# RWKV-7 and retention in one layer stack: an inverse whose blocks are turned on the chip, and a gate that is computed by tokens

## The chip, the cores and the metric

One core of a Trainium2 chip. The metric is the device time of one execution in microseconds; the kernel before was timed three times. Everything is float32; the large products run as fp32r, with each weight and each input split into a high and a low part. PE is the matrix engine (TensorE), DVE the vector engine (VectorE), ACT the scalar engine (ScalarE), SP the engine that issues most of the DMAs.

## What is computed

Three blocks on 256 tokens of width 1024. Block 1 is retention beside an RG-LRU; block 2 is local attention, convolution and pooling with an FFN; block 3 has two layers, each an FFN, a mixer, a cross attention and an FFN. The mixer of the first layer is RWKV-7, that of the second a gMLP. The three places that matter here, cut:

```python
# block 1
o_ret = group_norm_heads(chunkwise_retention(q, k, v)).reshape(B, T, RET_WIDTH)
y_ret = o_ret * jax.nn.silu(g_ret)
mixed = jnp.concatenate([y_ret, y_lru], axis=-1)      # times w_out
# RWKV-7: 16 heads of 64
g = jax.nn.sigmoid(xg @ g1) @ g2
def step(state, inp):                                 # over 256 tokens
    r_t, w_t, k_t, v_t, kk_t, b_t = inp
    sa = jnp.einsum('bhij,bhj->bhi', state, -kk_t)
    state = (state * w_t[:, :, None, :] + sa[..., None] * b_t[:, :, None, :]
             + v_t[..., :, None] * k_t[:, :, None, :])
    return state, jnp.einsum('bhij,bhj->bhi', state, r_t)
y = group_norm(y) * ln_w + ln_b
bonus = jnp.sum(r_h * k_h * r_k, axis=-1, keepdims=True) * v_h
return ((y + bonus) * g) @ w_o
# gMLP
u, v = jnp.split(jax.nn.gelu(h @ w_uv), 2, axis=-1)
v = rms_norm_3(v, v_norm)                             # then mixed over tokens by w_s
return (u * sv) @ w_o
```

## The kernel before

**The products.** A weight comes as blocks of 1 MB (128 x 2048) over SP's queue. Each half of a block is split on the chip: ACT casts it to the high part (L456), DVE subtracts for the low part (L459). `linear` works by features: per pair (m, k) two 128x256 products with the high and low part of the weight's column tile and one with the input's low part (L546 to L548), 3 x 8 x 8 = 192 for a 1024 x 1024 matrix. `linear_tok` works by tokens: 128x512 products (L563 to L565), 3 x 8 x 2 x 2 = 96 for the same matrix. Results stand in PSUM in banks of two kinds, "d" and "x", four of each, until ACT or DVE takes them out.

**The order.** Nothing is scheduled by a compiler: each engine runs its instructions in the order in which the Python text issues them, and an instruction that waits holds all behind it on its engine. `later(n, f)` puts f into the n-th step from now, `chain` spreads functions over the next steps, `soon` puts one behind the next step's products; `tick` and `tock` of a linear's step run what is due. `pump` issues loads and splits.

**Block 1.** The retention's output is computed by tokens (`orow`), normalized and left there. `in_gl` and `in_gr` are linears by features whose outputs go through `gate_out` (L1038): a product with the row factor r, Silu, a product with the LRU's output or with a tile of `orow` that PE has turned (`turned`, L1057, two 128x128 transposes a tile), and the split into high and low part of the input of `out1`.

**RWKV.** The state is carried over four pieces c of 64 tokens, for two halves of the heads (`chain(q)`, q = 0, 1). Within a piece a triangular system is solved with an inverse that is prepared for all 32 pairs (head, two pieces) at once. Its diagonal 32x32 blocks are made on DVE by forward substitution with one `column(s)` per column, 31 in all, on 128 partitions (`uy`: the first half u the triangles, the second y the inverse); they run among the steps of `rw_v`, four a step. `gather` (L1921) then writes y to DRAM and reads it back as `inv` with four DMAs (L1927), each block now a 32x32 tile across partitions; `inv` is cleared by POOL first. The off-diagonal block is made by `beside`: `across` (L1941) multiplies the coupling block with the block in place, `corner` (L1950) multiplies the result with the other block. `across` needs the first block transposed, which DVE does with eight 32x256 STREAM_TRANSPOSEs (L2158).

Around it stand, in the order of PE: the last products of `rw_v`, evicted by ACT into SV (`ev_v`, L2017); `direct(0)` and `direct(1)` of both chains (L2064); the output gate g (`gates`, four calls of 8 matmuls each, L1850 and L1851, evicted by ACT at L1852); `across` and `corner`; then the chain of pieces: for c = 0 to 3 `right` (R from the state, copied to Rs at L2072), `solve` (L2081) and `step` (new state, L2092 to L2094; outputs every second piece, `outs`). The group norm of the first half of the tokens (`normal(0)`) and its gating (`gated(m, 0)`) run within the chain by `later`. DVE makes the bonus products (`bonuses`, L1842) between the columns and the chain. The weights of `rw_o` follow at L2192 with the first result needed.

**gMLP.** After `gm_v` its output v (two tiles of 128x2048) is scaled by the norm's factor in four 128x1024 instructions (L374), then `gm_u` begins, whose steps use v as the products of `mix` from the second step on.

Of the kernel before, what the change touches and what calls it, by code (L numbers as in the profile page):

```python
# [172 lines left out]
def blocks_of(i):  # L173
# [128 lines left out]
class Net:  # L302
# [500 lines left out]
    def block1(self):  # L803
# [234 lines left out]
        def gate_out(k, ps, other):  # L1038
            g = self.tmp("t")
            nc.vector.tensor_mul(g, ps[:, :T], r)  # L1040
            o = {}

            def silu():
                o[0] = other()
                self.act(g, g, AF.Silu)

            def out():
                nc.vector.tensor_mul(g, o[0], g)
                self.split(g, yp.hi(k), yp.lo(k), lazy=True)
            self.chain(silu, out)  # L1050
        self.later(2, lambda: self.drop(th, w, rope))
        self.later(4, lambda: setattr(self, "keep", 2))
        self.linear("in_gl", xp, KD, 8, lambda m, ps: gate_out(m, ps, lambda: hl[:, m]), drain=False, late=0)
# [3 lines left out]
        def turned(m):  # L1057
            pt = self.psum("x")
            for t in range(2):
                nc.tensor.transpose(pt[:, t * P:(t + 1) * P], orow[:, t, m * P:(m + 1) * P], self.ident)  # L1060
            return pt[:, :T]
        self.linear("in_gr", xp, KD, 8, lambda m, ps: gate_out(8 + m, ps, lambda: turned(m)), late=0)
# [492 lines left out]
    def gmlp(self, st, nxt):  # L1555
# [19 lines left out]
        self.linear_tok("gm_v", xp, 4, ev_v, late=True)  # L1575
        sv, sr, sa = (self.tmp(n, 2, bufs=1) for n in ("sv", "sr", "sa"))
# [3 lines left out]
        for h in range(2):  # L1580
            for t in range(2):
                self.ts(v[t][:, h * D:(h + 1) * D], v[t][:, h * D:(h + 1) * D], sr[:, t:t + 1])
# [33 lines left out]
    def rwkv(self, st, nxt):  # L1616
# [221 lines left out]
        def bonuses(q, t):  # L1838
            for e in range(2):
# [81 lines left out]
        def gather():  # L1921
            inv.append(self.slot([P, 32, 64]))
            nc.gpsimd.memset(flat(inv[0]), 0.0)
            nc.sync.dma_start(dram[1], sq(uy[0][:, 1024:]))
            for n in (0, 2, 1, 3):
                s = blk[n]
                nc.sync.dma_start(inv[0][s, :, blk[n % 2]], dram[1][s].rearrange("q j t -> j q t"))  # L1927
        uy, inv = [], []

        def beside(i):  # L1930

            X = sq(uy[0][:, :1024])
# [3 lines left out]
            def across():  # L1936
                ps[0] = self.psum("x")
                for p in range(8):
                    hd, cp = divmod(8 * i + p, 2)
                    for n, c in ((0, 2 * cp + 1), (2, 2 * cp)):  # L1940
                        mm(ps[0][blk[n + 1], at(p)], Gh(hd)[blk[n], c, blk[n + 1]], X[blk[n], 8 * i + p],  # L1941
                           start=True, stop=True)
# [69 lines left out]
        self.later(3, lambda: zipped([lambda s=s: column(s) for s in range(31)] + [gather], 4))  # L2012
# [9 lines left out]
        nc.vector.tensor_copy(nn[:, 3], sums[0][:, 32:64].rearrange("p (s h) -> p s h", s=2))  # L2022
        bonus = nn[:, 3]
# [3 lines left out]
        for q in range(2):  # L2027
            for t in range(2):
                bonuses(q, t)

# [122 lines left out]
        for m in range(0, 8, 2):  # L2153
            gates(m)
        self.drop(*wl[1:])
# [15 lines left out]
        for c in range(4):  # L2171
            for f in range(1, 4):
                for ch in chains:
                    self.tick()
                    ch[f](c)
# [138 lines left out]
```

## Time and profile before

| | |
|---|---|
| median of 3 runs | 1789.21 us (1788.69 to 1789.83) |
| the profiled execution | 1788.29 us |
| its span, first to last instruction | 1786.3 us |
| mean granted clock of TensorE, share of full speed | 0.992 |
| PE busy | 1759.2 us, 98% of the span |
| DVE, ACT, POOL busy | 70%, 51%, 1% |
| DMA | 310.34 MB, mean 174 GB/s |

In the rows below a line of a timeline reads: start in us from the span's start, its length, engine, source line, operation, written and read tile, shape, number of instructions in the row, and in brackets the idle time ahead of it and the instruction whose end released it. A row of several instructions shows their sum in the second column or the stretch that they fill. A granted clock of 1.00 is 2.4 GHz, 0.50 is 1.2 GHz.

### The profile page before, as it was taken

Reading aid. Unit: us, or ns where it says so; the run is one execution under the profiler, and the core shown is the slowest. Engines: PE = TensorE matmul, PEld = TensorE weight load, DVE = VectorE, ACT = ScalarE, POOL = GpSimd, SP = SyncE. Lnnn points to the kernel's source line nnn. Section 1 sums busy time; section 2 is a strip of 40 time slices with the busy share of each in tenths; the row PEclk is TensorE's granted clock in tenths of the full one; section 3 lists DMA queues with packets and bytes.
Section 4 is the critical chain, followed back from the end, with each engine's and each line's share of the span. In section 5 each row is a group of like instructions: output and inputs, shape, how many; then the busy total and the mean of one; then the engine's idle time right before and its main releaser. Section 6 shows DMA issues by size and latency. Waiting matters only on the chain.

```text
span 1786.3 us, 27620 instructions
## 1 busy us (share of the span) xinstructions
PE 1759.2 (98%) x11142; PEld 1537.8 (86%) x11142; DVE 1252.6 (70%) x2292; ACT 914.1 (51%) x1550; POOL 9.8 (1%) x29
## 2 busy tenths in 40 slices
PE   8999999999999999999999999999999999999997
PEld 8899899899987888888688888888888899888886
DVE  7898888997757656678786865565556488675553
ACT  6878455665536544163235554444444555454451
POOL 0000000000000000000000000000000000000000
PEclk9999999999999999999989999999999999999999
DMA  8455445454653645603344454464445636345450
GB/s 321 143 189 202 170 157 216 165 185 166 211 207 129 210 173 185 258 25 119 96 167 163 168 188 165 165 236 170 162 181 191 240 119 236 142 169 185 165 189 24
DMA packets 55496, 310.34 MB, mean 174 GB/s; under 512 B 13728, under 2 KB 16841, under 8 KB 19145
## 3 DMA queue, kind: packets, MB, share of 16 engines
q1 hardware_dynamic: 54792, 304.39, 47.4%
q10 hardware_dynamic: 576, 4.19, 0.6%
q8 instruction: 87, 1.43, 0.3%
q14 instruction: 41, 0.33, 0.1%
HBM read 304.36 MB, written 4.21 MB: 173 GB/s over the span
## 4 chain that ended last, share of the span: by engine, by line
PE 89%; DVE 7%; ACT 2%; DMA 1%; issue 1%; SPq 0%; DVEq 0%; ACTq 0%
PE psd L544 17%; PE psd L548 14%; PE psd L563 10%; PE psd L565 10%; PE psd L564 10%; PE psd L546 6%; PE psd L547 6%; PE psx L544 2%; DVE s L459 2%; PE psd L2192 2%; PE psd L541 1%; PE psx L1455 1%; PE psx L548 1%; ACT s L367 1%; PE psx L1495 1%
## 5 line engine op out<-in xcount | busy, mean ns | idle before, releaser
L459 DVE TENSOR_TENSOR s<-s,s 128x1024 fp32r<-128x1024 f32 x524 | 627.1, 1220 | 169.3 <-ACT s L456 168.7
L548 PE MATMUL psd<-s,s 128*128 128x256 f32 x2336 | 655.8, 281 | 3.0 <-DVE s L459 2.8
L456 ACT CAST s<-s 128x1024 fp32r<-128x1024 f32 x524 | 532.1, 1046 | 180.0 <-PE psd L548 99.5
L544 PE MATMUL psd<-s,s 128*128 128x512 f32 x1392 | 491.2, 397 | 0.9 <-DVE s L630 0.9
L548 PEld LDWEIGHTS psd<-s,s 128*128 128x128 f32 x2336 | 442.8, 190 | 4.7 <-DVE s L459 4.2
L563 PE MATMUL psd<-s,s 128*128 128x512 f32 x816 | 323.7, 397 | 0.7 <-ACT s L367 0.7
L565 PE MATMUL psd<-s,s 128*128 128x512 f32 x816 | 318.6, 390 | 0.7 <-DVE s L370 0.7
L564 PE MATMUL psd<-s,s 128*128 128x512 f32 x816 | 317.8, 389 | 0.0
L544 PEld LDWEIGHTS psd<-s,s 128*128 128x128 f32 x1392 | 261.3, 188 | 63.4 <-DVE s L630 1.3
L546 PE MATMUL psd<-s,s 128*128 128x256 f32 x944 | 271.7, 288 | 1.0 <-ACT s L456 1.0
L547 PE MATMUL psd<-s,s 128*128 128x256 f32 x944 | 266.9, 283 | 0.0
L546 PEld LDWEIGHTS psd<-s,s 128*128 128x128 f32 x944 | 180.8, 192 | 2.7 <-ACT s L456 1.2
L565 PEld LDWEIGHTS psd<-s,s 128*128 128x128 f32 x816 | 153.1, 188 | 34.0 <-DVE s L370 1.3
L547 PEld LDWEIGHTS psd<-s,s 128*128 128x128 f32 x944 | 180.9, 192 | 0.1
L563 PEld LDWEIGHTS psd<-s,s 128*128 128x128 f32 x816 | 153.3, 188 | 31.2 <-ACT s L367 1.0
L564 PEld LDWEIGHTS psd<-s,s 128*128 128x128 f32 x816 | 153.4, 188 | 30.5
L1459 DVE TENSOR_TENSOR s<-psx,s 128x512 fp32r<-128x512 f32 x44 | 30.4, 691 | 94.7 <-ACT s L1461 79.2
L367 ACT ACTIVATE t<-psd,rc 128x256 f32<-128x256 f32 x88 | 41.5, 475 | 99.1 <-PE psd L565 96.7
L1461 ACT CAST s<-psx 128x512 fp32r<-128x512 f32 x40 | 23.5, 587 | 120.7 <-PE psx L1455 120.7
L370 DVE SCALAR_TENSOR_TENSOR t<-psd,rc,t 128x256 f32<-128x256 f32 x88 | 41.5, 482 | 47.5 <-ACT t L367 47.5
L367 ACT ACTIVATE t<-x 128x256 f32<-128x256 f32 x86 | 34.2, 407 | 68.4 <-DVE x L370 44.5
L367 ACT ACTIVATE s<-x,vecs 128x256 fp32r<-128x256 f32 (+1 forms) x80 | 40.2, 506 | 50.2 <-DVE x L1419 36.3
(382 smaller groups left out, 1818.1 us busy)
## 6 DMA issues: line engine op xcount, KB each, us to landing
s<-w_ffn_in SPq DMA_DIRECT2D x88, 1024.0 KB, 4.8
s<-w_ffn_out SPq DMA_DIRECT2D x44, 1024.0 KB, 4.7
s<-w_up SPq DMA_DIRECT2D x22, 1024.0 KB, 4.8
s<-w_out SPq DMA_DIRECT2D x12, 1024.0 KB, 5.0
s<-w_down SPq DMA_DIRECT2D x11, 1024.0 KB, 4.7
s<-w_xq SPq DMA_DIRECT2D x8, 1024.0 KB, 5.4
s<-w_xo SPq DMA_DIRECT2D x8, 1024.0 KB, 4.7
s<-w_gm_v SPq DMA_DIRECT2D x8, 1024.0 KB, 4.7
```

Of the source, the lines that this page charges most:

```text
L367: return self.nc.scalar.activation(out, in_, func, **kw)
L370: return self.nc.vector.scalar_tensor_tensor(out, in0, scalar, in1, op0=op0, op1=op1)
L456: self.nc.scalar.copy(hi, raw[:, s])
L459: self.nc.vector.tensor_sub(lo, raw[:, s], hi.bitcast(F32))
L544: mm(out, w[0], x.two(k), start=first, stop=False)
L546: mm(out[:, :T], w[0], x.hi(k), start=first, stop=False)
L547: mm(out[:, :T], w[0], x.lo(k), start=False, stop=False)
L548: mm(out[:, :T], w[1], x.hi(k), start=False, stop=last)
L563: mm(out, hi, w[0], start=first, stop=False)
L564: mm(out, hi, w[1], start=False, stop=False)
L565: mm(out, lo, w[0], start=False, stop=last)
L2192: mm(ps[:, :P], blocks[m // 2][j * P:(j + 1) * P][0], yo[:, k, o], start=k == 0, stop=k == KD - 1)
```

## The change

**Retention.** The weight of `in_gr` is laid out as that of `in_v`, and the linear is `linear_tok`. `ev_gr` takes a 128x512 bank out with Silu (ACT, the row factor as its scale) and multiplies it with `orow` (DVE). `turned` then turns the product with PE (16 transposes as before, in four banks of two tiles by two), ACT copies the high part and DVE subtracts for the low part, 128x2x256 each.

**gMLP.** A call of `_need` stands ahead of the scaling, for the first block of `gm_u`; in the built order no split moves by it. Of the four scalings those of the second half of v are put off by 3 and 4 steps.

**RWKV.** `gather` reads back only two of the four blocks by DMA. The whole y is transposed block by block on DVE into u (one 128x1024 STREAM_TRANSPOSE), from which `across` now reads; two more, 128x512, turn another view of y into two temporary tiles, and ACT copies the other two blocks from these into `inv` (four 32x512 copies, L1965 of the changed kernel). The eight 32x256 transposes go. The clearing of `inv` goes among the columns, the copy of the bonus too. `gates(0)` stands ahead of `across`, `gates(2)` behind `corner` and the first `right`, `gates(4)` and `gates(6)` at the pieces c = 1 and c = 2. Of the eight bonus products four stand between `across` and `corner`, four at steps of the chain. `normal(0)` runs in steps 12 to 18, `gated(m, 0)` in steps 19 to 24.

```diff
-        w[key] = _groups(part) if key == "in_v" else _tiles(part)
+        w[key] = _groups(part) if key in ("in_v", "in_gr") else _tiles(part)
...
+        def ev_gr(g, t, ps):
+            s = rows[t] = self.tmp("e", 512, bufs=4)
+            self.act(s, ps, AF.Silu, scale=rc[:, t:t + 1])
+            prod = lambda: nc.vector.tensor_mul(s, s, orow[:, t, g * 512:(g + 1) * 512])
...
+                for i in range(2):
+                    self.later(2 - g, lambda i=i: turned(g, i, pair))
+        def turned(g, j, s):
...
+                    nc.tensor.transpose(pt[:, i * T + t * P:i * T + (t + 1) * P], s[t][:, o:o + P], self.ident)
...
+            def out():
+                nc.scalar.copy(hi, both)
+                nc.vector.tensor_sub(lo, both, hi.bitcast(F32))
...
-        self.linear("in_gr", xp, KD, 8, lambda m, ps: gate_out(8 + m, ps, lambda: turned(m)), late=0)
+        self.linear_tok("in_gr", xp, 2, ev_gr, drain=False)
...
+                scaled = lambda v=v[t][:, h * D:(h + 1) * D], r=sr[:, t:t + 1]: self.ts(v, v, r)
+                if h:
+                    self.later(3 + t, scaled)
+                else:
+                    scaled()
...
         def gather():
-            inv.append(self.slot([P, 32, 64]))
-            nc.gpsimd.memset(flat(inv[0]), 0.0)
-            nc.sync.dma_start(dram[1], sq(uy[0][:, 1024:]))
-            for n in (0, 2, 1, 3):
-                s = blk[n]
-                nc.sync.dma_start(inv[0][s, :, blk[n % 2]], dram[1][s].rearrange("q j t -> j q t"))
+            u, y = uy[0][:, :1024], uy[0][:, 1024:]
+            d = [self.tmp("e", 512, bufs=4) for _ in range(2)]
+            nc.sync.dma_start(dram[1], sq(y))
+            nc.vector.transpose(u, y)
+            for n in (0, 2):
+                nc.sync.dma_start(inv[0][blk[n], :, blk[0]], dram[1][blk[n]].rearrange("q j t -> j q t"))
+            for i in range(2):
+                nc.vector.transpose(d[i], sq(y).rearrange("p j t -> p t j")[:, 16 * i:16 * i + 16])
+            for i in range(2):
+                for n in (1, 3):
+                    nc.scalar.copy(inv[0][blk[n], :, 32 + 16 * i:48 + 16 * i],
+                                   d[i][blk[n]].rearrange("p (t q) -> p q t", q=32))
...
-        for m in range(0, 8, 2):
-            gates(m)
...
-        for i in range(0, 32, 8):
-            for n in (0, 2):
-                nc.vector.transpose(uy[0][blk[n], 32 * i:32 * i + 256], inv[0][blk[n], i:i + 8, blk[0]])
+        gates(0)
         steps = [beside(i) for i in range(4)]
-        for n in range(2):
-            for st in steps:
-                st[n]()
+        for st in steps:
+            st[0]()
+        for q in range(2):
+            bonuses(q, 0)
+        for st in steps:
+            st[1]()
+        for ch in chains:
+            ch[1](0)
+        gates(2)
...
         for i, f in enumerate(normal(0)):
-            self.later(13 + i // 2, f)
+            self.later(12 + i, f)
         for m in range(8):
-            self.later(17 + m, lambda m=m: gated(m, 0))
+            self.later((19, 20, 21, 21, 22, 22, 23, 24)[m], lambda m=m: gated(m, 0))
+        for i, n in enumerate((3, 4, 9, 10)):
+            self.later(n, lambda i=i: bonuses(i % 2, 1, (i // 2,)))
...
+            if c in (1, 2):
+                gates(2 + 2 * c)
```

The order of ACT around the end of the columns, before. L2017 takes the products of `rw_v` out of the banks psd, L1852 the gate, L1944 the first result of `across`; psd_8432 and psd_8433 are the first 512 columns (heads 0 to 7, used by the chain q = 0) of both tiles of tokens, psd_8604 and psd_8605 the other 512 (heads 8 to 15, q = 1), which PE finishes last.

```order
L2017 COPY s_1063_8430<-psd_8432 64x512 x2
L2017 COPY s_1064_8431<-psd_8433 64x512 x2
L2017 COPY s_1063_8430<-psd_8604 64x512 x2
L2017 COPY s_1064_8431<-psd_8605 64x512 x2
L1852 COPY s_1133_8717<-psx_8718 128x512
L1852 COPY s_1133_8717<-psx_8724 128x512
L1852 COPY s_1133_8717<-psx_8730 128x512
L1852 COPY s_1133_8717<-psx_8736 128x512
L1944 COPY s_1069_8454<-psx_8750 32x256
```

And now. L2059 is the former L2017, L1879 the former L1852, L1983 the former L1944; L1965 are the new copies into `inv`.

```order
L2059 COPY s_1051_8298<-psd_8300 64x512 x2
L2059 COPY s_1052_8299<-psd_8301 64x512 x2
L1965 COPY s_1103_8491<-e_8518 32x32x16 x2
L1965 COPY s_1103_8491<-e_8519 32x32x16 x2
L2059 COPY s_1051_8298<-psd_8473 64x512 x2
L2059 COPY s_1052_8299<-psd_8474 64x512 x2
L1879 COPY s_1123_8584<-psx_8585 128x512
L1983 COPY s_1057_8322<-psx_8591 32x256
L1983 COPY s_1057_8322<-psx_8610 32x256
```

The four copies, which read the tiles that DVE turns behind the last column, now stand ahead of the last two evictions of `rw_v`.

The order of PE from the last matmuls of the gate on, before: L1850 and L1851 are `gates`, L1941 `across`, L1950 `corner`, L2081 the first `solve`.

```order
L1851 MATMUL psx_8736<-s_900_7405,s_899_7404 128x256
L1941 MATMUL psx_8750<-s_1069_8454,s_1017_8067 32x32 x16
L1941 MATMUL psx_8769<-s_1069_8454,s_1038_8209 32x32 x16
L1941 MATMUL psx_8788<-s_1069_8454,s_1052_8329 32x32 x16
L1941 MATMUL psx_8807<-s_1069_8454,s_1060_8414 32x32 x16
L1950 MATMUL psx_8826<-s_1122_8645,s_1069_8454 32x32 x16
L1950 MATMUL psx_8845<-s_1122_8645,s_1069_8454 32x32 x16
L1950 MATMUL psx_8864<-s_1122_8645,s_1069_8454 32x32 x16
L1950 MATMUL psx_8883<-s_1122_8645,s_1069_8454 32x32 x16
L2081 MATMUL psx_8909<-s_1124_8676,s_1122_8645 64x64
```

And now, again from the last matmuls of the first call of `gates` on: L1877 and L1878 are `gates`, L1980 `across`, L1989 `corner`.

```order
L1877 MATMUL psx_8585<-s_888_7273,s_887_7272 128x256
L1878 MATMUL psx_8585<-s_888_7273,s_887_7272 128x256
L1980 MATMUL psx_8591<-s_1057_8322,s_1005_7935 32x32 x16
L1980 MATMUL psx_8610<-s_1057_8322,s_1026_8077 32x32 x16
L1980 MATMUL psx_8629<-s_1057_8322,s_1040_8197 32x32 x16
L1980 MATMUL psx_8648<-s_1057_8322,s_1048_8282 32x32 x16
L1989 MATMUL psx_8671<-s_1103_8491,s_1057_8322 32x32 x16
L1989 MATMUL psx_8690<-s_1103_8491,s_1057_8322 32x32 x16
L1989 MATMUL psx_8709<-s_1103_8491,s_1057_8322 32x32 x16
L1989 MATMUL psx_8728<-s_1103_8491,s_1057_8322 32x32 x16
L1877 MATMUL psx_8751<-s_888_7273,s_887_7272 128x256
L1878 MATMUL psx_8751<-s_888_7273,s_887_7272 128x256
```

Only one of the four calls of `gates` is left ahead of `across`; the second (psx_8751) stands between `corner` and the first `solve`, and calls three and four (not shown) stand in the chain.

The order of DVE where `gm_u` begins, before: L374 are the scalings, L459 is the low part of a half block of weights, L1602 the first product of `gm_u` with the row factor.

```order
L374 TENSOR_SCALAR s_1672_13050<-s_1672_13050,sr_13349 128x1024
L374 TENSOR_SCALAR s_1673_13051<-s_1673_13051,sr_13349 128x1024
L374 TENSOR_SCALAR s_1672_13050<-s_1672_13050,sr_13349 128x1024
L374 TENSOR_SCALAR s_1673_13051<-s_1673_13051,sr_13349 128x1024
L459 TENSOR_TENSOR s_1709_13340<-s_1704_13291,s_1709_13340 128x1024
L1602 TENSOR_TENSOR t_13394<-psd_13365,rB_13044 128x256
```

And now (L1629 is the former L1602):

```order
L374 TENSOR_SCALAR s_1662_12917<-s_1662_12917,sr_13216 128x1024
L374 TENSOR_SCALAR s_1663_12918<-s_1663_12918,sr_13216 128x1024
L459 TENSOR_TENSOR s_1699_13207<-s_1694_13158,s_1699_13207 128x1024
L1629 TENSOR_TENSOR t_13259<-psd_13230,rB_12911 128x256
L459 TENSOR_TENSOR s_1706_13255<-s_1694_13158,s_1706_13255 128x1024
L1629 TENSOR_TENSOR t_13296<-psd_13261,rB_12911 128x256
L459 TENSOR_TENSOR s_1711_13288<-s_1697_13190,s_1711_13288 128x1024
L374 TENSOR_SCALAR s_1662_12917<-s_1662_12917,sr_13216 128x1024
```

Two of the scalings moved behind the first three low parts.

## Rows read from the trace of the kernel before

**Rows 1.** The page of the profile, its parts 1 and 2 (busy time; slices)

```profile
PE 1759.2 (98%) x11142; PEld 1537.8 (86%) x11142; DVE 1252.6 (70%) x2292; ACT 914.1 (51%) x1550; POOL 9.8 (1%) x29
...
PEclk9999999999999999999989999999999999999999
```

**Rows 2.** Waits of TensorE in the whole span: total us, times, longest us

```profile
PE psd L548 <- DVE s L459: 2.8, 4, 1.6
...
PE psx L2138 <- DVE s L2131: 1.1, 1, 1.1
...
PE psx L2081 <- ACT s L2072: 0.9, 1, 0.9
PE psd L2058 <- ACT s L2072: 0.9, 2, 0.4
```

**Rows 3.** Busy time by stretch, end of in_v and end of in_gl; columns in the first line

```profile
core 0: us, PE busy (x) PEld busy (x) DVE busy (x) ACT busy (x) POOL busy (x), PEclk, DMA share, GB/s
52.24:63.36 11.12, 11.12 (x50) 9.18 (x49) 5.14 (x8) 10.90 (x22) 0.00 (x0) 1.00 0.54 195
142.29:151.00 8.71, 8.71 (x75) 8.71 (x74) 7.50 (x22) 7.82 (x22) 0.00 (x0) 1.00 0.20 59
```

**Rows 4.** Timeline of VectorE, then of TensorE, where gm_u begins

```profile
1432.66 2.74 DVE L374 TENSOR_SCALAR s<-s,sr 128x1024 f32<-128x1024 f32 x4
1435.32 1.22 DVE L459 TENSOR_TENSOR s<-s,s 128x1024 fp32r<-128x1024 f32 x1
...
1434.67 0.28 PE L547 MATMUL psd<-s,s 128*128 128x256 f32 x1
1436.59 0.39 PE L548 MATMUL psd<-s,s 128*128 128x256 f32 x1 [1.64 <-DVE s L459]
```

**Rows 5.** Timeline of VectorE and SyncE queue around the end of the columns

```profile
869.08 0.21 DVE L1919 TENSOR_TENSOR s<-s,t 128x31 f32<-128x31 f32 x1
869.21 0.18 DVE L2022 COPY rwn<-psx 128x32 f32<-128x32 f32 x1
869.38 0.32 SPq L1924 DMA_DIRECT2D inv_dram<-s  x1
869.49 5.71 DVE L1842 TENSOR_TENSOR s<-s,rwn 64x512 f32<-64x512 f32 x8
...
875.23 3.69 DVE L2158 STREAM_TRANSPOSE s<-s 32x256 f32<-32x256 f32 x8
```

**Rows 6.** Timeline of ScalarE and TensorE in the same stretch

```profile
866.82 2.39 ACT L2017 COPY s<-psd 64x512 f32<-64x512 f32 x4 [11.34 <-PE psd L558]
...
867.58 2.08 PE L2064 MATMUL psd<-s,s 64*64 64x64 f32 x64
...
876.69 2.12 PE L1941 MATMUL psx<-s,s 32*32 32x32 f32 x98
...
```

**Rows 7.** Busy time by stretch of the RWKV layer, direct products to first rw_o product

```profile
867.57:869.59 2.02, 2.02 (x66) 1.95 (x65) 1.71 (x9) 1.60 (x3) 0.00 (x0) 1.00 0.00 0
869.59:876.69 7.10, 7.10 (x36) 5.99 (x33) 6.75 (x12) 1.76 (x3) 0.00 (x0) 1.00 0.70 148
876.69:882.72 6.03, 4.92 (x257) 4.48 (x256) 5.33 (x14) 3.95 (x11) 0.00 (x0) 0.95 0.02 5
882.72:888.90 6.18, 6.18 (x100) 5.89 (x104) 2.00 (x7) 0.98 (x3) 0.00 (x0) 0.50 0.99 369
888.90:899.10 10.20, 8.29 (x272) 7.41 (x276) 6.63 (x30) 2.60 (x7) 0.00 (x0) 1.00 0.68 235
899.10:909.40 10.30, 9.22 (x131) 7.70 (x124) 9.49 (x40) 2.04 (x5) 0.00 (x0) 0.50 0.44 164
909.40:916.50 7.10, 6.98 (x142) 5.68 (x139) 4.82 (x16) 3.66 (x11) 0.00 (x0) 1.00 0.01 3
```

**Rows 8.** The same view, the solve steps of piece 0 and of piece 1

```profile
882.72:886.85 4.13, 4.13 (x65) 3.96 (x65) 1.11 (x4) 0.69 (x3) 0.00 (x0) 0.50 0.97 345
891.09:893.12 2.03, 2.03 (x63) 1.96 (x63) 0.50 (x2) 0.38 (x1) 0.00 (x0) 1.00 0.16 61
```

More of the change, by code (lines that the diff above doesn't have):

```diff
@@ L1036, in block1, with gate_out @@
         yp = Pair(self, KD)
-        def gate_out(k, ps, other):
+        def gate_out(k, ps):
             g = self.tmp("t")
             nc.vector.tensor_mul(g, ps[:, :T], r)
[L1041 to L1045, printed above, removed]
             def out():
-                nc.vector.tensor_mul(g, o[0], g)
+                nc.vector.tensor_mul(g, hl[:, k], g)
                 self.split(g, yp.hi(k), yp.lo(k), lazy=True)
-            self.chain(silu, out)
+            self.chain(lambda: self.act(g, g, AF.Silu), out)
@@ L1051, in block1 @@
         self.later(2, lambda: self.drop(th, w, rope))
         self.later(4, lambda: setattr(self, "keep", 2))
-        self.linear("in_gl", xp, KD, 8, lambda m, ps: gate_out(m, ps, lambda: hl[:, m]), drain=False, late=0)
+        self.linear("in_gl", xp, KD, 8, gate_out, drain=False, late=0)
         yp.grow(KD)
         self.keep = 0
-        def turned(m):
-            pt = self.psum("x")
-            for t in range(2):
-                nc.tensor.transpose(pt[:, t * P:(t + 1) * P], orow[:, t, m * P:(m + 1) * P], self.ident)
-            return pt[:, :T]
@@ new lines, in turned @@
+        def turned(g, j, s):
+            pt = self.psum("x")
+            for i in range(2):
+                for t in range(2):
+                    o = (2 * j + i) * P
+                    nc.tensor.transpose(pt[:, i * T + t * P:i * T + (t + 1) * P], s[t][:, o:o + P], self.ident)
+            both, m = pt.rearrange("p (i t) -> p i t", i=2), 8 + 4 * g + 2 * j
+            hi, lo = yp.hi(m, 2), yp.lo(m, 2)
+            def out():
+                nc.scalar.copy(hi, both)
+                nc.vector.tensor_sub(lo, both, hi.bitcast(F32))
+            if g == 0:
+                self.soon(out)
+            else:
+                out()
@@ L1575, in gmlp @@
         self.linear_tok("gm_v", xp, 4, ev_v, late=True)
+        self._need(self.take_i, 0)
         sv, sr, sa = (self.tmp(n, 2, bufs=1) for n in ("sv", "sr", "sa"))
@@ L1581, in gmlp @@
             for t in range(2):
-                self.ts(v[t][:, h * D:(h + 1) * D], v[t][:, h * D:(h + 1) * D], sr[:, t:t + 1])
+                scaled = lambda v=v[t][:, h * D:(h + 1) * D], r=sr[:, t:t + 1]: self.ts(v, v, r)
+                if h:
+                    self.later(3 + t, scaled)
+                else:
+                    scaled()
         yp = Pair(self, 0)
@@ L1836, in lora2, with bonuses @@
             late_r[m] = with_r
-        def bonuses(q, t):
-            for e in range(2):
+        def bonuses(q, t, es=(0, 1)):
+            for e in es:
                 p, hs = slice(64 * e, 64 * e + 64), slice(8 * q, 8 * q + 8)
@@ L2011, in rwkv @@
             self.later(2 + m // 4, lambda m=m: by_tokens(m))
-        self.later(3, lambda: zipped([lambda s=s: column(s) for s in range(31)] + [gather], 4))
+        bonus = nn[:, 3]
+        self.later(5, lambda: nc.vector.tensor_copy(bonus, sums[0][:, 32:64].rearrange("p (s h) -> p s h", s=2)))
+        self.later(3, lambda: zipped([lambda s=s: column(s) for s in range(24)] + [room_inv]
+                                 + [lambda s=s: column(s) for s in range(24, 31)] + [gather], 4))
         def ev_v(gr, t, ps):
```

25 lines of the change are left out of this document (15 added, 10 removed).

## The prediction

> **What bounds the kernel now.** I read the page first: TensorE is busy 98% of the span, VectorE 70%, ScalarE 51%, and the granted clock dips once in forty slices [rows 1]. So time can only be won where TensorE waits or runs slowly, and a change on the other engines counts only if TensorE waits for it. Second, the waits of TensorE: the largest that this change touches sum to single microseconds. For the low part of a split, 2.8 in four waits, one of 1.6; in the chain of pieces, 1.1 for the new state and 0.9 and 0.9 for ScalarE's copy of R [rows 2]. Third, timelines and stretches of the three places. Measurement noise sets what counts: 0.2%, or 3.6 us, is about what a measurement of this kernel can tell from no change.
>
> The sum is made against the profiled execution, 1788.29 us; the median, 1789.21, lies 0.92 above it, and I add that at the end.
>
> **Retention: -1.0 us.** The products change from 192 of 256 columns to 96 of 512. The nearest rows: the last half of `in_v`, 48 wide products (50 records with two others), 11.12 us; the last three eighths of `in_gl`, 72 narrow ones (75 records), 8.71 us [rows 3]. Scaled by 96/48 and 192/72, 22.24 and 23.23: -1.0. The 16 transposes stay. ScalarE's and VectorE's work per output gets less (banks of 512 for 256), and in the `in_gl` stretch they are at 7.82 and 7.50 of 8.71, so nothing gets in the way there. The second group is turned in the first step of `out1`; its parts are needed at that linear's fourth quarter of inputs, some 9 us of TensorE work later by the 8.71 of these rows, against a transpose, a copy and a subtraction. The third `out1` load now stands on SP behind the load of the memory, and is covered by the blocks already split. Bounds: -1.4 if the two late steps of the old `gate_out` had also waited; +0.3 if the wide products come no cheaper and the last two turned banks stop TensorE once.
>
> **gMLP: -1.3 us.** Four scalings take 2.74, 0.68 each, directly ahead of a low part of 1.22; TensorE waits 1.64 for that [rows 4]. Two scalings less ahead of it let it end 2 x 0.68 = 1.37 earlier, some of it lost to DVE's own latency between instructions: -1.3. The two that are put off stand behind the third low part, and the first use of the second half of v is eight steps away. `_need` moves no split. Bounds: -1.64, the whole wait; 0, if the next split is late instead.
>
> **RWKV: +4.5 us.** Here the order of ScalarE decides. Before, its four copies of the last `rw_v` products begin at 866.82, after idling 11.34 us for TensorE, and the direct products run at 867.58 without a stop [rows 6]. Now four copies into `inv` stand ahead of them. These need the tiles that VectorE turns after the last column. So the products of chain 1, half of `direct`, wait for VectorE. Step by step:
> - The last column ends at 869.29 (869.08 + 0.21), the bonus copy of 0.18 went ahead among the columns [rows 5]: 869.47.
> - Three transposes. No row has them wide. A VectorE pass over 128x1024 took 1.22 [rows 4], one over 512 elements 0.71 (5.71/8), and a transpose of 256 elements 0.46 (3.69/8) [rows 5]. By size from the passes: 1.22 + 2 x 0.71, the first small tile at 871.4, the second at 872.1. If instead they go as the 256-element transposes, four of these for the large and two for each small: 1.84 + 2 x 0.92, the second tile at 873.2. I take the passes, nearest in size.
> - Four copies on ScalarE at 0.60 (2.39/4 for 64x512) [rows 6]. From the first tile at 871.4: 873.8. Then two evictions for the first tile of tokens, 1.2: 875.0 (874.1 if the copies, on 32 partitions, take less; 875.5 if the transposes are slow).
> - TensorE is free at 868.6, half of the 2.02 of `direct` in [rows 7]. It waits 6.4 us (5.5 to 6.9).
> - Then the rest of `direct` 1.0; the first quarter of the gate, 7.10/4 = 1.77; `across` and `corner`, 6.03 with 4.92 busy, of whose 1.11 idle some 0.85 stood for the eight transposes that go: 5.2 [rows 7]. Now four bonus products of 0.71 stand on VectorE ahead of `corner`'s evictions, 2.8 us; about half is covered by `corner` itself, so the second quarter of the gate waits some 1.3 for a bank, begins at 884.3 and ends at 886.1. The first `solve` starts at 886.2 where it started at 882.72: +3.5.
> - The chain, 33.75 us from 882.72 to 916.47 by the stretches of [rows 7], takes the two remaining quarters of the gate, 3.54. Its idle time is 3.1 (10.20 - 8.29, 10.30 - 9.22, 7.10 - 6.98); the waits of 1.1 and 0.9 are at piece borders, where one of the quarters stands now. I take 2.5 of the 3.54 as covered: +1.0 (0.4 if the idle takes nearly all, 3.5 if none). The bonus products moved into the chain and the later group norm lie on VectorE, busy 2.00 of 6.18 and 6.63 of 10.20 there.
>
> Nothing else enters: the two remaining DMA blocks of the inverse are wanted only by the first `solve`, 13 us after the store; the clearing of `inv` is on an engine busy 1%.
>
> **A rule that speaks against the change.** ScalarE idled 11.34 us behind a single wait while other work was queued [rows 6], so an instruction that waits holds all behind it. The Trainium skill says it for ScalarE, VectorE and GpSimd alike ("TensorE: Matmul & The Clock Gate", table at its head): strict FIFO queues, only TensorE has a partial reorder window. By the row the RWKV term is +4.5; were ScalarE able to take the ready evictions first, the 6.4 would go and the term would be -1.9, the total 1785.0.
>
> **Sum.** -1.0 - 1.3 + 4.5 = +2.2: profiled 1790.5, median 1791.4. Taking all lower bounds: -1.4 - 1.64 + (4.5 - 0.9 - 0.6) = 0, 1789.2. Taking all upper ones: 0.3 + 0 + (4.5 + 0.5 + 2.5) = +7.8, 1797.0.
>
> **Rivals.**
> - *The stop slows TensorE* (slower). The granted clock was 0.50 from 882.72 to 888.90, behind a stretch in which TensorE was busy 4.92 of 6.03 with 32x32 products [rows 7]; the same solve steps took 4.13 there and 2.03 at 1.00 [rows 8]. A stop of 6.4 us is a far emptier stretch. If the clock falls behind it and falls again in the chain as before, one more such stretch is paid: half of 6.18 to half of 9.22, 3.1 to 4.6, taken as 3.9: 1795.3. It decides from the point at which the stop adds a slow stretch rather than moving one forward. For it: the emptiness. Against it: the gate's full-size products then stand between and may bring the clock back before the chain. The Trainium skill's rule bears on this ("TensorE: Matmul & The Clock Gate", Part 1: The HAM clock gate): the throttled state is the default, and activity releases it. The two levels in the rows agree with that. Chance 0.30.
> - *The gate among the chain keeps the clock up* (faster). Both slow stretches of the chain, 6.18 and 9.22 busy at 0.50 [rows 7], would halve if the 128x256 products spread among them hold the clock: -7.7, 1783.7; only one of them, -3.1 or -4.6, 1787 to 1788. For it: the stretch with the gate ran at 1.00. Against it: one quarter at a time is 1.77 us among 8 to 10 us of small products. Chance 0.17, most of it for both.
> - *The gMLP part does nothing* (it doesn't do what it says): the split that was meant to be ahead was there already, and the next low part is late by as much. +1.3: 1792.7. Chance 0.05.
>
> **How the numbers follow.** The forecast has the remaining 0.48, centred on 1791.4 with its bounds 1789.2 to 1797.0. No change means 1785.6 to 1792.8. The forecast lies inside it for about three quarters of its chance (0.36), and beyond it for 0.12; the slow rival lies mostly beyond (0.25 of 0.30), the fast one mostly below (0.14 of 0.17), the third inside. That gives faster 0.14, same 0.49, slower 0.37. The range runs to 1797.5 above, the sum of upper bounds and some of the slow rival, and to 1785.0 below, which takes the single-stretch case of the fast rival and leaves the double one out.
>
> **What would show it.** Right: a wait of 5.5 to 6.9 us of TensorE for ScalarE's last evictions of `rw_v`, ahead of half of the direct products; the first `solve` 3 to 4 us later in the RWKV layer; `in_gr` 1 us shorter; 0.3 in place of 1.64 at `gm_u`. Wrong: no wait there; slow stretches in the granted clock at other places, or more or fewer than two in this layer; a new wait in `out1` or in the chain for VectorE over 1 us.

## The result, and the profile after

The changed kernel took 1804.22 us in the median, against 1789.52 us for the kernel before in the same comparison: a ratio of 1.0076, 95% interval 1.0063 to 1.0089, some 14 us slower. The forecast was 1791.4, no change being the likeliest; the range ended at 1797.5. (One execution of the four stood far outside all others, at 8717 us and a granted clock of 0.187; the median counts it and the ratio does not, and the other three took 1803.40 to 1804.73.) The profiled execution took 1804.73 us, span 1802.9.

The page of the profile after, the rows that answer to [rows 1]:

```profile
PE 1768.9 (98%) x11046; PEld 1540.8 (85%) x11046; DVE 1247.5 (69%) x2271; ACT 916.5 (51%) x1546; POOL 9.8 (1%) x29
...
PEclk9999999999999999999789999999999999999999
```

TensorE is still busy 98% of a longer span: busy time itself grew by 9.7 us though the kernel has 96 products less. That already says that it ran slower, and the clock's row dips further in the slices of the RWKV layer.

The waits of TensorE after the change (total us, times, longest), which answer to [rows 2]:

```profile
PE psd L2100 <- ACT s L2059: 7.7, 1, 7.7
PE psx L2128 <- DVE s L374: 2.0, 2, 1.7
...
PE psd L548 <- DVE s L459: 1.5, 4, 0.8
...
PE psx L1877 <- DVE s L374: 1.0, 1, 1.0
```

There is one wait of 7.7, at the second half of the direct products, and a new one of 1.7 in the chain of pieces. The gate's second quarter waits 1.0 for a bank, forecast 1.3. The wait for low parts fell from 2.8 to 1.5: the gMLP's step, where 1.64 became 0.31, as forecast.

Busy time by stretch from the first direct product to the first `rw_o` product, the columns as in [rows 3]; the rows answer to [rows 7]. In order: direct products of chain 0; the stop; direct products of chain 1; first quarter of the gate; `across` and `corner`; second quarter; first solve; then the chain up to the first `rw_o` product.

```profile
868.17:869.30 1.13, 1.13 (x33) 1.01 (x32) 0.99 (x5) 0.00 (x0) 0.00 (x0) 1.00 0.00 0
869.30:876.99 7.69, 0.02 (x2) 0.00 (x1) 3.54 (x6) 4.79 (x6) 0.00 (x0) 0.72 0.38 102
876.99:879.49 2.50, 2.37 (x33) 2.06 (x33) 0.00 (x0) 1.71 (x3) 0.00 (x0) 0.50 0.00 0
879.49:883.12 3.63, 3.63 (x9) 2.52 (x9) 0.00 (x0) 0.00 (x0) 0.00 (x0) 0.52 0.00 0
883.12:890.15 7.03, 7.03 (x257) 6.89 (x256) 4.01 (x8) 3.15 (x8) 0.00 (x0) 0.73 0.02 5
890.15:894.82 4.67, 3.71 (x8) 2.52 (x8) 3.25 (x8) 1.01 (x3) 0.00 (x0) 0.50 0.00 0
894.82:897.64 2.82, 2.82 (x65) 2.75 (x64) 0.42 (x1) 0.96 (x2) 0.00 (x0) 0.68 0.62 177
897.64:909.13 11.49, 10.19 (x268) 8.93 (x265) 7.21 (x23) 2.82 (x7) 0.00 (x0) 1.00 0.57 208
909.13:917.40 8.27, 6.12 (x126) 5.21 (x123) 6.71 (x41) 2.45 (x6) 0.00 (x0) 0.98 0.72 276
917.40:934.53 17.13, 15.76 (x191) 12.45 (x191) 9.81 (x27) 4.41 (x13) 0.00 (x0) 0.51 0.17 70
```

The sum is 66.36 us where the seven stretches of [rows 7] sum to 48.93: 17.4 us more. Idle time of TensorE is 13.6 in place of 4.2, so 9.4 of it are waits. The rest, 8.1, is busy time, nearly all of it by the low clock: by the same records the chip granted 0.50 from 872.74 to 882.98, from 886.39 to 896.63 and from 917.11 to 934.18, 37.6 us in three stretches, where before it were 17.1 in two. TensorE was busy in 30.6 of the 37.6 and in 15.3 of the 17.1, and half of the difference is 7.6. Outside the layer the profile after has one more stretch at 0.50, 3.4 us long at 552 us, which neither the profile before nor that of run 4 has; it is worth 1.7 us of this one execution.

The timelines around the stop: VectorE, ScalarE, TensorE, with rows that answer to [rows 5] and [rows 6].

```profile
869.61 0.21 DVE L1946 TENSOR_TENSOR s<-s,t 128x31 f32<-128x31 f32 x1
869.85 1.25 DVE L1958 STREAM_TRANSPOSE s<-s 128x1024 f32<-128x1024 f32 x1
871.02 1.92 DVE L1962 STREAM_TRANSPOSE e<-s 128x512 f32<-128x512 f32 x2
...
887.82 2.79 DVE L1869 TENSOR_TENSOR s<-s,rwn 64x512 f32<-64x512 f32 x4
890.64 1.43 DVE L374 TENSOR_SCALAR s<-psx 32x256 f32<-32x256 f32 x4
```

```profile
872.11 4.22 ACT L1965 COPY s<-e 32x512 f32<-32x512 f32 x4 [16.06 <-DVE e L1962]
876.36 2.38 ACT L2059 COPY s<-psd 64x512 f32<-64x512 f32 x4
```

```profile
868.17 1.15 PE L2100 MATMUL psd<-s,s 64*64 64x64 f32 x32
876.99 2.57 PE L2100 MATMUL psd<-s,s 64*64 64x64 f32 x32 [7.67 <-ACT s L2059]
...
917.40 1.12 PE L2128 MATMUL psx<-s,s 128*64 128x64 f32 x14 [1.65 <-DVE s L374]
```

The last column ends at 869.82. The wide transpose takes 1.25, the two others 0.96 each, and ScalarE's four copies begin at 872.11 after 16 us of waiting, 1.06 each; only then come the evictions, and TensorE goes on at 876.99. Later the four bonus products (887.82, line L1869) stand ahead of `corner`'s evictions (890.64).

Retention, from the end of the retention's own last products among those of `in_gl` to the same product of `out1`, before and then after:

```profile
142.29:172.80 30.51, 30.51 (x252) 30.15 (x250) 26.02 (x57) 25.52 (x57) 0.00 (x0) 1.00 0.57 209
```

```profile
142.01:171.26 29.25, 29.25 (x155) 25.05 (x154) 19.23 (x36) 21.82 (x46) 0.00 (x0) 1.00 0.52 189
```

30.51 became 29.25: -1.3.

### The profile page after: what moved, and what is told of

Its sections match the earlier page's. It is cut to its first block, busy times and chain, and to the rows that moved or that the text cites. A ratio compares the mean times of both kernels' runs of the same rounds, so it can differ in the third digit from the quotient of the medians.

```text
span 1802.9 us, 27383 instructions
## 1 busy us (share of the span) xinstructions
PE 1768.9 (98%) x11046; PEld 1540.8 (85%) x11046; DVE 1247.5 (69%) x2271; ACT 916.5 (51%) x1546; POOL 9.8 (1%) x29
## 4 chain that ended last, share of the span: by engine, by line
PE 89%; DVE 7%; ACT 2%; DMA 1%; issue 1%; SPq 0%; DVEq 0%; ACTq 0%
PE psd L544 17%; PE psd L548 14%; PE psd L563 10%; PE psd L565 10%; PE psd L564 10%; PE psd L546 5%; PE psd L547 5%; PE psx L544 2%; PE psd L2236 2%; DVE s L459 1%; PE psd L541 1%; PE psx L1477 1%; PE psx L548 1%; ACT s L367 1%; PE psx L1517 1%
## 5 line engine op out<-in xcount | busy, mean ns | idle before, releaser
L459 DVE TENSOR_TENSOR s<-s,s 128x1024 fp32r<-128x1024 f32 x524 | 627.0, 1220 | 170.9 <-ACT s L456 170.4
L548 PE MATMUL psd<-s,s 128*128 128x256 f32 x2272 | 638.9, 281 | 1.7 <-DVE s L459 1.5
L544 PE MATMUL psd<-s,s 128*128 128x512 f32 x1392 | 492.5, 398 | 0.8 <-DVE s L630 0.8
L548 PEld LDWEIGHTS psd<-s,s 128*128 128x128 f32 x2272 | 431.1, 190 | 3.4 <-DVE s L459 2.9
L563 PE MATMUL psd<-s,s 128*128 128x512 f32 x848 | 337.0, 397 | 0.6 <-ACT s L367 0.6
L565 PE MATMUL psd<-s,s 128*128 128x512 f32 x848 | 331.7, 391 | 0.7 <-DVE s L370 0.7
L564 PE MATMUL psd<-s,s 128*128 128x512 f32 x848 | 331.1, 390 | 0.0
L544 PEld LDWEIGHTS psd<-s,s 128*128 128x128 f32 x1392 | 261.4, 188 | 63.7 <-DVE s L630 1.2
L546 PE MATMUL psd<-s,s 128*128 128x256 f32 x880 | 253.3, 288 | 0.4 <-ACT s L456 0.4
L547 PE MATMUL psd<-s,s 128*128 128x256 f32 x880 | 248.9, 283 | 0.0
L565 PEld LDWEIGHTS psd<-s,s 128*128 128x128 f32 x848 | 159.6, 188 | 35.4 <-DVE s L370 1.3
L563 PEld LDWEIGHTS psd<-s,s 128*128 128x128 f32 x848 | 159.6, 188 | 32.6 <-ACT s L367 1.0
L564 PEld LDWEIGHTS psd<-s,s 128*128 128x128 f32 x848 | 159.9, 189 | 31.8
L546 PEld LDWEIGHTS psd<-s,s 128*128 128x128 f32 x880 | 168.6, 192 | 2.1 <-ACT s L456 0.6
L547 PEld LDWEIGHTS psd<-s,s 128*128 128x128 f32 x880 | 168.7, 192 | 0.1
```

The lines of the kernel that those rows point to most:

```text
L459: self.nc.vector.tensor_sub(lo, raw[:, s], hi.bitcast(F32))
L544: mm(out, w[0], x.two(k), start=first, stop=False)
L546: mm(out[:, :T], w[0], x.hi(k), start=first, stop=False)
L547: mm(out[:, :T], w[0], x.lo(k), start=False, stop=False)
L548: mm(out[:, :T], w[1], x.hi(k), start=False, stop=last)
L563: mm(out, hi, w[0], start=first, stop=False)
```

## The experiments

Ratios are to the kernel before on the same chip, with their 95% intervals; 0.001 is 1.8 us. Lines of kernels differ a little; the names tell which is meant.

**1. The four copies behind the last evictions.** `gather` keeps the transposed tiles, and the copies are issued after `rw_v` has been drained.

```diff
-            for i in range(2):
-                for n in (1, 3):
-                    nc.scalar.copy(inv[0][blk[n], :, ...], d[i][blk[n]]...)
+            turned_blocks.extend(d)
...
         self.drain()
+        copied()
```

> The changed kernel, with the four ScalarE copies into the inverse moved behind the last evictions of rw_v; the gate stays spread. Theory A (the stop of TensorE behind those copies, and the low clock that follows it, are all of what the RWKV layer lost): no wait ahead of the second half of the direct products, but one of about 3.5 us at the first results of across, whose evictions now stand behind the copies; granted clock full from the direct products to the first solve; time 1789 to 1794. Theory B (the gate's full-size products no longer stand as one block ahead of the small products, and this lets the clock fall): low clock through across, corner, solve and again late in the chain, time 1797 to 1802.

Measured: 1794.06 us, ratio 1.0018 (1.0008 to 1.0028). The stop is gone. What is left of it is a wait at `across`:

```profile
PE psx L1984 <- ACT s L1879: 2.0, 1, 2.0
```

Ten us came back by the order of four instructions. Theory A says more than B, but not all: the low clock still ran from 871.74 to 881.98, which A had not expected, and from 905.87 to 919.52.

**2. The gate ahead of `across`, the copies as in the change.**

```diff
-        gates(0)
+        for m in range(0, 8, 2):
+            gates(m)
+        self.drop(*wl[1:])
...
-        gates(2)
...
-            if c in (1, 2):
-                gates(2 + 2 * c)
```

> The changed kernel, with all four calls of the gate ahead of across, as before the change; the ScalarE copies stay ahead of the last evictions, so the stop stays. Theory A: the stop of 7.7 us stays, the gate's block runs at the low clock for some 5 to 10 us behind it, and the time is 1799 to 1803. Theory B: the block brings the clock back ahead of the small products and the chain runs as before; time 1794 to 1797.

Measured: 1803.05 us, ratio 1.0070 (1.0054 to 1.0086). This is the upper end of what A expected: with the stop in place, where the gate stands hardly matters.

**3. Both.**

> Both edits: copies behind the last evictions of rw_v, and the whole gate ahead of across. Both theories: no stop, granted clock as before the change, across without a wait; the RWKV layer about 1 us shorter than before the change (eight transposes less ahead of across), and the gains of retention and gMLP kept: 1785 to 1788. If a third cause (the later group norm, the bonus products among the chain) costs time by itself, the chain from the first solve to the first rw_o product is longer than its former 33.75 us and the time above 1789.

Measured: 1792.88 us, ratio 1.0011 (1.0002 to 1.0020). Above what both theories allowed, so there was a third cause. Its profile shows two places. TensorE and VectorE at the first solve:

```profile
883.60 0.34 PE L2122 MATMUL psx<-s,s 64*64 64x64 f32 x1 [2.42 <-issue]
```

```profile
880.26 2.79 DVE L1869 TENSOR_TENSOR s<-s,rwn 64x512 f32<-64x512 f32 x4
883.08 1.43 DVE L374 TENSOR_SCALAR s<-psx 32x256 f32<-32x256 f32 x4
```

The solve waits 2.4 us for `corner`'s evictions (L374), which stand behind the four bonus products (L1869) on VectorE. The view puts that wait down to "issue"; VectorE's rows show what ended with it. And the chain takes 38.87 us (883.60 to 922.47) where it took 33.75.

**4. Retention and gMLP alone**: the first three pieces of the diff on the kernel before.

> The kernel before with the retention part and the gMLP part of the change alone. Both theories: the RWKV layer as before; retention -1.0 to -1.5, gMLP -1.2: 1786.5 to 1787.5. If these parts cost something elsewhere (the stretch at 552 us that the changed kernel ran at half clock), 1788 to 1789.5.

Measured: 1786.74 us, ratio 0.9979 (0.9970 to 0.9989), and faster than both kernels. Its RWKV layer, to the first solve and from there to `rw_o`:

```profile
864.08:879.96 15.88, 14.35 (x354) 12.73 (x353) 13.81 (x33) 7.30 (x17) 0.00 (x0) 0.95 0.33 68
879.96:913.27 33.31, 28.63 (x625) 24.54 (x625) 22.89 (x89) 9.25 (x25) 0.00 (x0) 0.82 0.53 192
```

**5. As 3, the bonus products back between the last column and the chain.**

```diff
-        for q in range(2):
-            bonuses(q, 0)
...
-        for i, n in enumerate((3, 4, 9, 10)):
-            self.later(n, lambda i=i: bonuses(i % 2, 1, (i // 2,)))
...
         bv = self.slot([P, 2, D])
+        for q in range(2):
+            for t in range(2):
+                bonuses(q, t)
```

> The run with both edits (copies behind, gate in front), and the eight bonus products back between the last column and the chain, beside the gate. Theory C1 (the four bonus products between across and corner hold corner's evictions on VectorE, and the first solve waits 2.4 us for them): that wait goes, first solve 2 to 2.5 us earlier after the direct products, time about 2 to 3 us under the run with both edits, ratio 0.999 to 1.0005. Theory C2 (only the later group norm and gating cost, by a longer stretch at the low clock at the chain's end): no gain, ratio 1.001.

Measured: 1792.23 us, ratio 1.0007 (0.9996 to 1.0018). The wait of 2.4 is gone, and hardly any time with it: `across` and `corner` now run into the low clock (0.85 on the way to the solve), and the chain is still long.

```profile
868.38:885.51 17.13, 16.22 (x353) 14.84 (x353) 13.57 (x27) 11.36 (x21) 0.00 (x0) 0.85 0.18 48
885.51:922.47 36.96, 31.89 (x625) 27.28 (x625) 22.79 (x89) 9.12 (x26) 0.00 (x0) 0.75 0.47 173
```

**6. As 5, the group norm and gating at their former steps.**

```diff
-            self.later(12 + i, f)
+            self.later(13 + i // 2, f)
...
-            self.later((19, 20, 21, 21, 22, 22, 23, 24)[m], lambda m=m: gated(m, 0))
+            self.later(17 + m, lambda m=m: gated(m, 0))
```

> As the run with the bonus products back, and group norm and gating of the first tokens at their former steps: of the RWKV part only the transposes on the chip are left, with their copies behind the last evictions. Theory C1 and C2 both hold: the chain is back at 33 to 34 us, the direct products to the first solve take 14 to 15 us (before 15.15), and the time is that of retention and gMLP alone or up to 1 us less: ratio 0.997 to 0.998. If the on-chip transposes cost by themselves (copies of 1.08 us each, transposes of 1.0 us): ratio 0.999 to 1.001.

Measured: 1787.81 us, ratio 0.9984 (0.9974 to 0.9994).

```profile
866.40:883.41 17.01, 16.15 (x353) 14.84 (x352) 13.42 (x27) 11.37 (x21) 0.00 (x0) 0.85 0.18 48
883.41:916.70 33.29, 28.64 (x625) 24.50 (x625) 22.93 (x89) 9.23 (x26) 0.00 (x0) 0.82 0.52 192
```

The chain is back from 36.96 to 33.29. The way to the first solve is not the expected 14 to 15 us: it takes 17.01, part of it at the low clock, against 15.15 before the change. In run 5, VectorE and TensorE show where the later group norm is met in the chain; `gn` are the factor's small instructions, nine in 1.9 us (the first, the last three and what stands behind them are shown):

```profile
903.67 0.17 DVE L374 TENSOR_SCALAR gn<-bag 128x16 f32<-128x16 f32 x1
...
904.93 0.59 DVE L370 SCALAR_TENSOR_TENSOR gn<-gn 128x16 f32<-128x16 f32 x3
905.55 0.43 DVE L374 TENSOR_SCALAR s<-psx 64x256 f32<-64x256 f32 x1
```

```profile
906.04 0.68 PE L2136 MATMUL psx<-s,s 128*64 128x64 f32 x14 [1.66 <-DVE s L374]
```

One step later, the factor stands ahead of the second chain's solve eviction (L374, 905.55), and the state product of the third piece waits 1.66. But at the former steps, in run 6, the same instructions and the two that follow delay the first gating transposes, by more:

```profile
904.70 0.66 PE L2182 MATMUL psx<-misc,s 128*128 128x128 f32 x2 [2.13 <-DVE s L2175]
```

So the wait that moved is not the cost. By the two rows of stretches TensorE stands idle in the chain for 5.07 us in run 5 (36.96 - 31.89) and 4.65 in run 6 (33.29 - 28.64); 3.25 of the 3.67 are busy time. The low clock makes it: it ran from 907.54 to 921.19 in run 5, and from 902.12 to 908.95 in run 6. Why the stretch is longer with the later group norm, these traces do not show.

**7. As 6, the gate spread as in the change.**

> The changed kernel with the copies behind the last evictions, the bonus products and the group norm as before the change; the gate stays spread over the chain. Theory B' (spreading the gate costs by itself, since the block of full-size products is missing ahead of the small ones): low clock from across to the first solve, 4 to 6 us slower than with the gate in front, ratio 1.000 to 1.001. Rival (the gate fills waits in the chain): as fast as with the gate in front, ratio 0.997 to 0.998.

Measured: 1789.53 us, ratio 0.9994 (0.9985 to 1.0004). No gain from the gate in the chain: its two quarters make the chain 33.78 us in place of 33.29, and a stretch of 6.8 us at the low clock stays in it. Between 6 and 7 lie 0.0010, between 1 and 3 0.0007, between the change and 2 0.0006, each time against the spread gate and each time within the intervals: 1 to 2 us. The chain of run 7:

```profile
884.21:917.99 33.78, 29.67 (x641) 24.83 (x641) 22.24 (x86) 10.76 (x27) 0.00 (x0) 0.90 0.50 189
```

**8. As 6, the copies ahead of the evictions again**: the stop alone.

> The same kernel as the one with the chain back as before the change, but with the four copies again ahead of the last evictions of rw_v: the stop alone. Theory A: the stop of 7 to 8 us and a stretch at the low clock behind it that costs 3 to 5 us more: 10 to 13 us over that kernel, ratio 1.003 to 1.005. If the gate's block takes the clock back at once, only the stop: 7 to 8 us over it, ratio 1.001 to 1.002.

Measured: 1800.07 us, ratio 1.0051 (1.0034 to 1.0069), 0.0067 or 12 us over run 6. Wait and stretches, to be read against those of run 6:

```profile
PE psd L2103 <- ACT s L2059: 7.8, 1, 7.8
```

```profile
864.77:891.76 26.99, 18.21 (x353) 16.21 (x352) 13.30 (x27) 12.26 (x22) 0.00 (x0) 0.76 0.11 30
891.76:924.97 33.21, 28.94 (x625) 24.81 (x625) 22.84 (x89) 9.23 (x26) 0.00 (x0) 0.84 0.53 192
```

The chain is the same (33.21 and 33.29); all of the loss lies ahead of the first solve, 26.99 against 17.01. The wait is 7.8; busy time grew by 2.1 ahead of the solve (18.21 against 16.15) by the low clock. The medians are 12.3 apart, the profiled executions only 7.1: this one is the fastest of four (1795.22), and run 6's had a stretch of 3.4 us at the low clock at 776 us that this one has not. The three others took 1799.92 to 1800.74 at a mean granted clock of 0.990 against 0.992 here, which within the rounding is 2 to 4 us of time. So in most executions the clock costs more than in the profiled one, some 4 us.

**9. As 6, with `across` reading its blocks densely.** In run 6 the 32 columns that a product of `across` reads lie 32 elements apart.

```diff
-            nc.vector.transpose(u, y)
+            nc.vector.transpose(u.rearrange("p (q j) -> p j q", j=32), sq(y))
...
-            X, XT = ..., uy[0][:, :1024].rearrange("p (j q) -> p q j", j=32)
+            X, XT = ..., sq(uy[0][:, :1024])
```

> The kernel with the chain back as before the change and the copies behind the last evictions, but the first transpose writes its blocks so that across reads the 32 columns of a block next to each other (before: 32 elements apart). Theory S (TensorE reads a moving operand with columns 128 bytes apart slower: 29.8 ns a 32x32 product against 21.6 before the change): across takes 2.8 us or less in place of 3.4, the time falls by 0.6 to 1 us, ratio 0.997 to 0.9984. Rival (across is slowed by something else, such as ScalarE's copies beside it): across stays at 3.4 us, ratio unchanged at 0.9984. The transpose itself may take longer (1.3 to 2 us), which lies beside the gate.

Measured: 1788.71 us, ratio 0.9986 (0.9977 to 0.9995). `across` of run 6, then of this one, then its wide transpose:

```profile
875.52 3.63 PE L1984 MATMUL psx<-s,s 32*32 32x32 f32 x122
```

```profile
876.67 2.21 PE L1984 MATMUL psx<-s,s 32*32 32x32 f32 x128 [0.52 <-ACT s L1879]
```

```profile
868.72 1.96 DVE L1958 STREAM_TRANSPOSE s<-s 128x1024 f32<-128x1024 f32 x1
```

The products are faster, 17.3 ns each (2.21/128) in place of 29.8 (3.63/122). But the transpose that writes the blocks apart takes 1.96 in place of 1.25, ScalarE's copies start later by that, and `across` waits for its banks. The cost moved to another engine; no time is gained.

**10. As 9, the last quarter of the gate behind `corner`.**

> As the run with dense blocks, and the last of the four calls of the gate behind corner and the first copies of R, the other three ahead of across. If full-size products just ahead of the first solve shorten the stretch at the low clock and cover corner's evictions: direct products to the first solve unchanged at 16 to 17 us, solve steps of the first piece 2 us shorter, ratio 0.996 to 0.9975. If not: 1 us of new wait at across, whose banks ScalarE frees later than before, ratio 0.998 to 0.999.

Measured: 1788.52 us, ratio 0.9987 (0.9978 to 0.9995). It only moves: `across` waited 1.5 us for its banks, as the second case expected, and the low clock fell on `corner` and on the quarter itself (875.40 to 882.23) instead of on the solve.

**11. Run 4 again, beside 9 and 10.**

> The kernel before with the retention and gMLP parts alone, a second time beside the two others on one chip: ratio 0.997 to 0.9985. If the dense blocks make the transposes on the chip worth having, it lies above theirs by 0.0003 to 0.001; if not, at or below.

Measured: 1786.16 us, ratio 0.9979 (0.9970 to 0.9989), the figure of run 4. With dense reads or without, the transposes on the chip do not pay; the differences to runs 6, 9 and 10 (0.0005 to 0.0008) lie inside the intervals.

**12. Run 4 with the last quarter of the gate behind `corner` and the first copies of R.**

> The kernel before with the retention and gMLP parts, and one piece of the RWKV part: the last of the four calls of the gate behind corner and the first copies of R. If the full-size products there shorten the stretch at the low clock of the first piece and stand where TensorE waits 0.9 us for the copies of R: the layer 1 to 2 us shorter, ratio 0.9965 to 0.9975. If they only move: the same as without that piece, 0.9979. If the transposes ahead of across, no longer covered by a whole gate, are then waited for: up to 1.8 us of wait at across, ratio 0.998 to 0.999.

Measured: 1788.64 us, ratio 0.9986 (0.9977 to 0.9994): not better. `across` waited for the old transposes (0.67 and four times 0.16 to 0.23), no longer covered by a whole gate. None of the runs is better than run 4, which beats both kernels.

## Why the prediction was wrong

The parts, each as the difference of two runs that differ in that piece (for the transposes also in the clearing, the copy of the bonus and the first copies of R, which moved with them):

| part | ratio | us |
|---|---|---|
| the stop (8 against 6) | +0.0067 | +12 |
| later group norm and gating (5 against 6) | +0.0023 | +4 |
| bonus products moved (3 against 5) | +0.0004 | +0.7 |
| gate spread (change against 2) | +0.0006 | +1 |
| transposes on the chip, in the old order (6 against 4) | +0.0005 | +1 |
| retention and gMLP (4) | -0.0021 | -4 |

They sum to +0.0084, the whole is +0.0076; the rest lies inside the intervals. The first two and the last are clear of noise, the three small ones are not. Beside the other pieces the stop is worth a little less, 0.0058 (change against 1) and 0.0059 (2 against 3).

**Retention and gMLP** were right: -1.3 and -1.3 in the traces, forecast -1.0 and -1.3. Runs 4 and 11 gained 3.8 (2.0 to 5.4, which holds the 2.3); of the 4.2 us between the profiled spans some 1.7 came from a stretch at 776 us that was at the low clock in the profile of before and not in that of run 4. That is no effect of these parts: the profiles of runs 3, 5, 6 and 7 have both parts and that stretch.

**The stop** was named, at its place and with its cause: ScalarE's order. Its length was mis-sized. "Four copies on ScalarE at 0.60" took the time of a dense 64x512 copy; these read elements 32 apart and took 1.06, 1.8 us more in all. Two transposes at 0.71 took 0.96. Some 0.9 of this was made good: the last column ended 0.5 us after TensorE was free and not 0.9, and TensorE went on after the first of the two evictions that the sum had it wait for. So 6.4 (5.5 to 6.9) became 7.7. "By size from the passes" held for the dense transpose (1.25 against 1.22) and not for the others.

**What follows the stop** is the step that failed most. The sum carried the work behind it at the full clock: direct products 1.0, quarter of the gate 1.77, `across` and `corner` 5.2. They took 2.50, 3.63 and 7.03, the second quarter of the gate with its wait 4.67 in place of 3.1, and the first solve came 26.65 after the first direct product, not 18.6 (886.2 - 867.58): 1.3 by the longer stop and 6.8 behind it. The low clock is most of the 6.8; some 0.6 are the reads of `across` (below). I had this as a rival of 0.30 with a price of 3.9, "one more such stretch". The layer has 20.5 us more at the low clock, costing 7.6, and the mechanism belonged in the forecast: a stop of 6 us is longer than any other wait of TensorE in the trace. The clock fell while it lasted (at 872.74 in the profile after, at 868.54 in run 8). The rule that the rival cited (the Trainium skill, "TensorE: Matmul & The Clock Gate", Part 1: The HAM clock gate) would have put it so: throttled is the default. The trace agrees, 0.50 in the middle of the stop.

**The chain.** The sum had +1.0 (0.4 to 3.5) for the gate's two quarters, and nothing for the later group norm and the bonus products, since VectorE was busy 6.63 of 10.20 there. It became 39.71 for 33.75, +6.0. The quarters were not far off, 0.5 in run 7 against 6. The term put at nothing failed: run 5 against 6 puts 3.7 of the chain on the later group norm and gating, and a share of busy time did not tell that. It is not the chance of one execution. In the five kernels that have them later (the change and runs 1, 2, 3 and 5) the chain takes 37.0 to 39.7 us and ends in a stretch of 13.7 to 17.1 at the low clock; in the nine others it takes 31.2 to 33.8, and the stretch 6.8 to 10.2. Two of my signs of being wrong came: a third slow stretch in the layer, and a new wait for VectorE of over 1 us in the chain, 1.65; by run 6 it is not that wait that costs.

Together: 8.0 to the first solve and 5.0 in the chain, less 0.3 for retention, and 1.7 for the stretch at 552 us, come to 14.4; the profiled 1804.73 lies 14.2 above its forecast of 1790.5.

**The fast rival** (the gate among the chain keeps the clock up) fell in run 7. **The rival that gMLP does nothing** fell with the wait of 1.5. **The -0.85 for the eight old transposes** was a misreading. Of the 1.11 us of idle time in that stretch 0.85 end with ScalarE's copy of R, ahead of the first solve (the first line, from TensorE's timeline before); TensorE waited 0.2 for the transposes (the second, from its waits before).

```profile
882.72 0.48 PE L2081 MATMUL psx<-s,s 64*64 64x64 f32 x2 [0.85 <-ACT s L2072]
```

```profile
PE psx L1941 <- DVE s L2158: 0.2, 1, 0.2
```

And the little that there was to gain was given back: `across` with blocks read 32 apart takes 3.4 us where it took 2.8, and the clock falls in it.

Not settled: how the later group norm and gating lengthen the slow stretch at the chain's end, and which of the two does it, since they were moved together. Of the stop's 12 us, 7.8 are the wait; the profiled execution shows 2 of clock, the medians leave 4, and that these are the clock too rests on the mean granted clocks of run 8, not on a trace.

## What to carry to other kernels

Before a copy is moved to another engine, look at what stands behind it in that engine's queue: an instruction that waits for the end of a chain must stand behind every eviction that TensorE needs sooner. Price a stop of TensorE with what comes after it, not by its length alone: here 7.8 us of waiting cost 12. And idle time on an engine is no reason to put moved instructions at nothing: here they cost 4 us, and only the run that put them back alone showed it.

## What was not expected of the hardware

- **Reads with a stride.** A copy of 32x512 on ScalarE whose elements lie 32 apart took 1.06 us; a dense one of 64x512 took 0.60. A transpose of 128x1024 on VectorE took 1.25 with dense sides and 1.96 with its blocks written 32 apart. TensorE's 32x32 products took 29.8 ns with columns 32 elements apart and 17.3 ns dense (the row of 98 in [rows 6], 21.6 each, holds a pause). The Trainium skill has the rule ("SBUF — State Buffer", Door 1: The DMA port swizzle, the note on cache lines): in float32 a stride is free up to 4 elements, beyond it each access pays. The runs have only the stride of 32 and agree with it. For VectorE and TensorE run 9 against 6 changes the layout alone; ScalarE's two copies also differ in shape and source, so there the stride as the cause is not shown. The prediction had not taken it into account.
- **A low clock spreads.** Moving the bonus products back took away a wait of 2.4 us (run 5) and gained under 1 us, since the low clock then fell on other work; so did the quarter of the gate in runs 10 and 12. In this layer a wait that goes is no gain before the clock's rows have been read behind it.
